# Eight experts on one core: three in plain fp32, woven between the five in split fp32

## The chip, the core and the metric

The kernel runs on one core of a Trainium2 chip, as one program. Its time is the device time of one execution in microseconds (us). Before the change it is 2560.36 us, the median of three runs (2557.41, 2560.36 and 2562.28).

Four engines matter here. TensorE (PE in the profile; its weight loads are PEld) multiplies out of SBUF into PSUM. VectorE (DVE) and ScalarE (ACT) do the elementwise work and bring PSUM back to SBUF. SyncE (SP) issues the DMAs that bring the weights from HBM, in the order of its queue.

## The reference

The model has two blocks of two layers each, on 256 tokens of width 1024. All but the last part is the same in both kernels and is not shown. The last part of the last layer is a mixture of eight experts, of which each token uses two:

```python
def moe_swiglu(h, router, w_gate, w_up, w_down):          # 8 experts, hidden width 3584
    t = h.reshape(-1, d)                                   # 256 tokens x 1024
    logits = (t @ router).astype(jnp.float32)
    top_v, top_i = lax.top_k(logits, TOP_K)                # TOP_K = 2
    top_w = jax.nn.softmax(top_v, axis=-1)
    gates = jnp.sum(jax.nn.one_hot(top_i, N_EXPERTS, dtype=jnp.float32) * top_w[..., None], axis=1)
    for e in range(N_EXPERTS):
        y_e = (jax.nn.silu(t @ w_gate[e]) * (t @ w_up[e])) @ w_down[e]
        out = out + gates[:, e:e + 1] * y_e
```

Each expert has three weight matrices of 1024 x 3584 fp32, 44 MB. All eight are read whole, 352 MB in all.

## The kernel before, in words

The kernel sorts the experts by the number of tokens that chose them. The first five places hold up to 128 tokens each, the last three up to 64 (`PLACES`); a branch at the end, which repeats the computation for tokens that didn't fit, is built into the program. `moe_gather` collects an expert's tokens with one-hot matmuls, `moe_places` transposes the one-hot matrix for the way back, and `combine` adds an expert's output to `acc`, scaled by the gate.

`moe_lane` is a generator. It walks through a list of experts, each in four steps over the hidden width (1024, 1024, 1024 and 512). A step takes its tokens through the gate matrix (`half(i, "gate")`), puts the SiLU into SBUF (`gate`), goes through the up matrix, multiplies (`inner`), transposes the product (`turn`) and takes it through the down matrix (`down`). The gate and up of step i + 1 stand ahead of the down of step i. It yields after each weight buffer. A weight buffer is 128 partitions x 2048 fp32, 1 MiB, and an expert has 42.

There are two kinds of experts:

- A wide one (places 0 to 4, 128 tokens) works in split fp32. `weights` (L211 to L229) loads a raw buffer, ScalarE casts it into a buffer wh (L227) and VectorE subtracts wh from raw into a buffer wl (L228). The raw buffer is then free. `mm3` makes three matmuls of each product (L242 to L244): twelve of 128x512 per weight buffer, each with 128 columns of the array.
- A tight one (places 5 to 7, 64 tokens) works in plain fp32. `whole_weights` (L231 to L237) loads a buffer, and TensorE reads it as it is, in four matmuls per weight buffer that use 64 columns each (L2307 for gate and up, L2364 for down). The profile counts each of these as two. The buffer is free when TensorE has read it.

The buffers of a kind form a ring: the code asks for them in turn, and the ring has five of raw and three each of wh and wl in this part of the kernel (`phase(2, 2, 48)`, `wider(raw=2, wh=1, wl=1)`, `wider(raw=1)`). A DMA can be issued when the buffer five turns earlier is free. The tight experts, which need no wh or wl, take the buffers of all three kinds in the order of `KINDS`, eleven in all.

PSUM has two pools of four banks, "a" and "b". Results of gate and up lie in "a", two banks for a wide expert and one for a tight one. Gathers, transposes, the results of down and the combines lie in "b".

`moe_pass` runs one lane over `TOGETHER`, the groups (0), (1, 2), (3, 4) and (5, 6, 7), so the five wide experts come first and the three tight ones last. A scheduler then sets the order of each engine's instructions by priority, near the order of the code.

Of the kernel before, what the change touches and what calls it, by code (L numbers as in the profile page):

```python
# [3 lines left out]

# [9 lines left out]
F32R = mybir.dt.float32r  # L14
# [8 lines left out]
D = 1024  # L23
# [5 lines left out]
def f(ap):  # L29
    return ap.bitcast(F32)  # L30
# [25 lines left out]
class Core:  # L56
# [171 lines left out]
                nc.vector.tensor_sub(L[:, c:e], raw[:, c:e], f(H[:, c:e]))  # L228
        return v(H), v(L)  # L229

    def whole_weights(s, src, k0, nk, c0, cn, rows="k p", kind="raw"):  # L231

        s.n += 1
        raw = s.buffer(kind)
        v = f(raw)[:, :nk * cn].rearrange("p (k c) -> p k c", k=nk)
        s.nc.sync.dma_start(v, src[k0:k0 + 128 * nk, c0:c0 + cn].rearrange(f"({rows}) c -> p k c", p=128))
        return v  # L237

# [1750 lines left out]
class MoE:  # L1989
# [192 lines left out]
                s.nc.sync.dma_start(s.out[t * 128:t * 128 + 128, c * 512:c * 512 + 512].rearrange(  # L2182
                    "p (d w) -> p d w", d=2), s.acc(t, c))

    def moe_gather(s, N, slot, js, places):


        nc = s.nc
        wide = places[js[0]] == 128
        n = len(js) * (2 if wide else 1)  # L2190
        j0, j1 = js[0], js[-1] + 1
        if wide:
            sl = s.small([128, 2, 4], "slotu")
            nc.vector.tensor_tensor(sl[:, :, :n].rearrange("p t (j u) -> p t j u", u=2),
                                    slot[:, :, j0:j1, None].to_broadcast([128, 2, j1 - j0, 2]),
                                    s.off[:, None, None, :].to_broadcast([128, 2, j1 - j0, 2]), op=OP.subtract)
            sl = sl[:, :, :n]
        else:
            sl = slot[:, :, j0:j1]
        P = s.t2([128, 2, 256], "onehot", F32R)  # L2200
        W = n * 64
        for t in range(2):
            nc.vector.tensor_tensor(P[:, t, :W].rearrange("p (u c) -> p u c", c=64), bc(s.slots[:, :64], n),
                                    sl[:, t, :, None].to_broadcast([128, n, 64]), op=OP.is_equal)
        X = []
        for d in range(0, ND, 2):
            p = s.psum("b")
            for m in range(2):
                for h, src in enumerate((N.H, N.L)):
                    for t in range(2):  # L2210
                        nc.tensor.matmul(p[:, m * W:m * W + W], src[d // 2][:, t, m * 128:m * 128 + 128], P[:, t, :W],
                                         start=(h == 0 and t == 0 and m == 0), stop=(h == 1 and t == 1),
                                         skip_group_check=True)
            if not wide:
                y = s.t2([128, 2, W], "xf")
            for m in range(2):
                v, g = p[:, m * W:m * W + W], s.col("ln_ffn_2", 8 + d + m)
                if wide:
                    x = s.t2([128, 512], "xe", F32R)[:, :2 * W].rearrange("p (a j c) -> p j a c", a=2, j=len(js))
                    v = v.rearrange("p (j c) -> p j c", j=len(js))  # L2220
                    nc.scalar.activation(x[:, :, 0], v, AF.Copy, scale=g)
                    nc.vector.scalar_tensor_tensor(x[:, :, 1], v, g, f(x[:, :, 0]), op0=OP.mult, op1=OP.subtract)
                    X.append(x)
                else:
                    nc.scalar.activation(y[:, m], v, AF.Copy, scale=g)
                    X.append(y[:, m].rearrange("p (j c) -> p j c", c=64))
        return {j: [X, i, places[j], P] for i, j in enumerate(js)}

    def moe_places(s, N, G):

        nc = s.nc
        rc = s.small([128, len(G)], "slotrc")
        p = s.psum("b")
        Y = []
        for X, i, n, P in G.values():
            y = P[:, :, i * n:i * n + n]
# [8 lines left out]
        nc.vector.tensor_copy(rc, p[:, :len(G)])  # L2245
        for g, y in zip(G.values(), Y):
            PT = s.t2([128, 2, 128], "onehotT", F32R)
            p = s.psum("b", dt=F32R)
            for t in range(2):
                nc.tensor.transpose(p[:, t * 128:t * 128 + 128], y[:, t], s.identR)  # L2250
            nc.scalar.copy(PT, p[:, :256].rearrange("p (t c) -> p t c", t=2))
# [1 line left out]

    AHEAD = 3
    WIDE = 1024
    KINDS = ("raw", "wh", "raw", "wl", "raw", "wh", "raw", "wl", "raw", "wh", "wl")

    def moe_weights(s, i):

# [1 line left out]

    def moe_pass(s, N, first, ahead):

        for _ in s.moe_lane(N, N.slot, s.PLACES, s.TOGETHER, first, ahead, True):
            pass

    def moe_lane(s, N, slot, places, together, G, ahead=(), most=False):


        nc = s.nc  # L2270
# [6 lines left out]
        py = {}  # L2277
        ahead = list(ahead)
        src = {nm: I[f"o_moe_w_{nm}_2"][0] for nm in ("gate", "up", "down")}
        kinds = itertools.cycle(s.KINDS)  # L2280

        def weights(nm, j, *a):
            e = N.expert[j]
            w = src[nm]
            w = w[e] if isinstance(e, int) else w[bass.ds(e, 1)].rearrange("o r c -> (o r) c")
            return s.weights(w, *a) if places[j] == 128 else s.whole_weights(w, *a, kind=next(kinds))

        def half(i, nm):

# [36 lines left out]
        def turn(i, h):  # L2326
# [2 lines left out]
            wide = G[steps[i][0]][2] == 128  # L2329
            out = []  # L2330
            for x in h:
                p = s.psum("b")
                n = x.shape[1] // 128
                for k in range(n):
                    nc.tensor.transpose(p[:, k * 128:k * 128 + 128], x[:, k // 2 * 256 + k % 2:k // 2 * 256 + 256:2],
# [32 lines left out]
        def combine(j):  # L2368
# [5 lines left out]
            for c in range(2):  # L2374
# [1 line left out]
                    yH, yL = s.t2([128, 512], "eyH", F32R), s.t2([128, 512], "eyL", F32R)  # L2376
                    s.split(py[j][c], yH, yL)
                for t in range(2):
                    p = s.psum("b")
                    if wide:  # L2380
                        mm(p, PT[:, t, :], yH, start=True, stop=False)
                        mm(p, PT[:, t, :], yL, start=False, stop=True)
# [6 lines left out]
        pg = yield from half(0, "gate")  # L2389
        if most:  # L2390
            s.moe_rms(N)
        s.moe_places(N, G)
        h = gate(0, pg)
        h = inner(0, h, (yield from half(0, "up")))
        for i in range(n):
            j, f0, fn = steps[i]
            if f0 == s.WIDE and i + per < n and steps[i + per][0] not in G:
                g = s.moe_gather(N, slot, next(x for x in together if steps[i + per][0] in x), places)
                s.moe_places(N, g)
                G |= g  # L2400
            pg = (yield from half(i + 1, "gate")) if i + 1 < n else None
            hs = turn(i, h)
# [62 lines left out]
```

## Time and profile before

The profile is of one execution; spans are from the first to the last instruction.

| | before |
|---|---|
| time of the profiled execution | 2560.47 us |
| its span | 2558.8 us |
| median of three runs | 2560.36 us |
| TensorE busy | 2382.6 us, 93% of the span |
| VectorE, ScalarE busy | 1679.8 us (66%), 1287.6 us (50%) |
| moved by DMA | 559.56 MB, 219 GB/s over the span |

In the profile's slices of 64 us each, TensorE stands at nine tenths or more nearly everywhere up to the last six slices, where it falls to seven or eight. The transfers rise from some 150 GB/s to about 350 GB/s at 1600 us, where the experts begin, and to about 410 GB/s in the last six slices. A share of busy time is an average; for what a stage is worth one reads which engine or transfer the others wait for in that stage. A matmul's busy time includes the time in which it passes through the array, which overlaps with the next one, so the distance of two starts says more than a duration. PEclk is the clock that TensorE was granted: 1.00 is 2.4 GHz.

### The profile page before, as it was taken

The page shows a single profiled execution, that of the slowest core. Times are in us where ns is not written, and L with a number is a line of the kernel's source. Part 1 is how long each engine was busy: PE and PEld are TensorE (multiplying, and loading weights), DVE is VectorE, ACT ScalarE, POOL GpSimd, SP SyncE. Part 2 cuts the span into 40 slices and gives each one's busy share as a digit, 9 for nine tenths or more (in the row PEclk, how much of TensorE's full clock was granted, in tenths as well). Part 3 has the DMA queues.
Part 4 walks back from the last instruction along what each step waited for, and adds up shares of the span by engine and source line. Part 5 has one row for each costly group of instructions (what it writes and reads, how often), then busy time and mean ns, then how long its engine had stood idle before and what let it go on. Part 6 is the DMA issues. An engine that isn't in the chain of part 4 may idle for free.

```text
span 2558.8 us, 39340 instructions
## 1 busy us (share of the span) xinstructions
PE 2382.6 (93%) x15516; PEld 2000.3 (78%) x15516; DVE 1679.8 (66%) x2974; ACT 1287.6 (50%) x2124; POOL 88.6 (3%) x180
## 2 busy tenths in 40 slices
PE   7988799999999999989999998999999999987786
PEld 6877689999888999879999898887888777632222
DVE  6876486658886765666657886888898988610000
ACT  4554265445555644664445553777777776510000
POOL 2011010000001000000000000000000000000000
PEclk9998699999999999989999998999999999999999
DMA  5310355555435455525554322899999998899998
GB/s 163 118 59 34 38 178 165 183 167 164 132 116 166 129 189 170 177 67 182 185 166 144 100 67 83 306 336 353 369 348 345 347 363 326 341 410 409 411 412 330
DMA packets 266191, 559.56 MB, mean 219 GB/s; under 512 B 12751, under 2 KB 172510, under 8 KB 251662
## 3 DMA queue, kind: packets, MB, share of 16 engines
q1 hardware_dynamic: 264544, 555.71, 61.3%
q0 software_dynamic: 1328, 1.22, 0.9%
q8 instruction: 124, 2.03, 0.3%
q14 instruction: 69, 0.57, 0.1%
q10 hardware_dynamic: 126, 0.03, 0.0%
HBM read 555.88 MB, written 1.05 MB: 218 GB/s over the span
## 4 chain that ended last, share of the span: by engine, by line
PE 71%; DMA 11%; DVE 8%; issue 4%; ACT 3%; POOL 2%; SPq 0%; ACTq 0%; POOLq 0%; DVEq 0%
PE pa L243 16%; PE pa L244 16%; PE pa L242 16%; DVE wl L228 3%; PE pb L243 3%; PE pb L244 2%; PE pb L242 2%; DMA raw<-in_o_moe_w_down_dram 2%; DMA wl<-in_o_moe_w_down_dram 2%; PE pb L1180 2%; PE pb L1805 2%; DMA wh<-in_o_moe_w_down_dram 2%; ACT wh L227 1%; PE pa L2307 1%; PE pb L1494 1%
## 5 line engine op out<-in xcount | busy, mean ns | idle before, releaser
L228 DVE TENSOR_TENSOR wl<-raw,wh 128x512 fp32r<-128x512 f32 (+1 forms) x982 | 974.4, 1021 | 204.3 <-ACT wh L227 199.9
L227 ACT CAST wh<-raw 128x512 fp32r<-128x512 f32 (+1 forms) x982 | 826.1, 888 | 549.7 <-issue 266.3
L242 PE MATMUL pa<-xH,wh 128*128 128x256 f32 (+1 forms) x1936 | 553.1, 286 | 16.0 <-ACT xH L326 8.1
L244 PE MATMUL pa<-xH,wl 128*128 128x256 f32 (+1 forms) x1936 | 552.9, 286 | 1.0 <-DVE wl L228 1.0
L243 PE MATMUL pa<-xL,wh 128*128 128x256 f32 (+1 forms) x1936 | 553.1, 286 | 0.6 <-DVE xL L327 0.5
L242 PEld LDWEIGHTS pa<-xH,wh 128*128 128x128 f32 (+1 forms) x1936 | 372.4, 193 | 18.2 <-ACT xH L326 8.8
L243 PEld LDWEIGHTS pa<-xL,wh 128*128 128x128 f32 (+1 forms) x1936 | 372.2, 192 | 3.5 <-DVE xL L327 2.0
L244 PEld LDWEIGHTS pa<-xH,wl 128*128 128x128 f32 (+1 forms) x1936 | 372.2, 192 | 2.9 <-DVE wl L228 1.9
L243 PE MATMUL pa<-wl,xe 128*128 128x512 f32 x560 | 220.9, 395 | 7.7 <-DVE wl L228 7.7
L244 PE MATMUL pa<-wh,xe 128*128 128x512 f32 x560 | 219.4, 392 | 0.0
L2323 DVE SCALAR_TENSOR_TENSOR eh<-pa,slotrc,eh 128x512 f32<-128x512 f32 (+1 forms) x47 | 33.4, 733 | 267.1 <-PE pa L2307 259.4
L242 PE MATMUL pa<-wh,xe 128*128 128x512 f32 x560 | 207.7, 393 | 0.0
L242 PE MATMUL pa<-hidH,wh 128*128 128x256 f32 x528 | 149.4, 283 | 0.0
L243 PE MATMUL pa<-hidL,wh 128*128 128x256 f32 x528 | 149.4, 283 | 0.0
L244 PE MATMUL pa<-hidH,wl 128*128 128x256 f32 x528 | 149.4, 283 | 0.0
L243 PEld LDWEIGHTS pa<-wl,xe 128*128 128x128 f32 x560 | 105.6, 189 | 33.9 <-DVE wl L228 12.8
L244 PEld LDWEIGHTS pa<-wh,xe 128*128 128x128 f32 x560 | 105.6, 189 | 21.1
L242 PEld LDWEIGHTS pa<-wh,xe 128*128 128x128 f32 x560 | 105.4, 189 | 21.2
L243 PE MATMUL pb<-wl,ehH 128*128 128x512 f32 x280 | 112.2, 401 | 1.5 <-DVE wl L228 1.5
L244 PE MATMUL pb<-wh,ehL 128*128 128x512 f32 x280 | 110.3, 394 | 0.0
L242 PE MATMUL pb<-wh,ehH 128*128 128x512 f32 x280 | 102.0, 393 | 2.5 <-ACT wh L227 2.5
L2317 ACT ACTIVATE eh<-pa,slotrc 128x512 f32<-128x512 f32 (+1 forms) x47 | 30.7, 674 | 145.3 <-PE pa L2307 125.8
(818 smaller groups left out, 3870.5 us busy)
## 6 DMA issues: line engine op xcount, KB each, us to landing
raw<-in_o_moe_w_down_dram SPq DMA_DIRECT2D x91, 1024.0 KB
raw<-in_o_moe_w_up_dram SPq DMA_DIRECT2D x89, 1024.0 KB
raw<-in_o_moe_w_gate_dram SPq DMA_DIRECT2D x88, 1024.0 KB
raw<-in_ffn_w_dram SPq DMA_DIRECT2D x60, 1024.0 KB
raw<-in_od_w_in_dram SPq DMA_DIRECT2D x20, 1024.0 KB
raw<-in_o_w_in_dram SPq DMA_DIRECT2D x16, 1024.0 KB
wl<-in_o_moe_w_gate_dram SPq DMA_DIRECT2D x13, 1024.0 KB
wh<-in_o_moe_w_up_dram SPq DMA_DIRECT2D x13, 1024.0 KB
```

The source lines that it names most:

```text
L227: nc.scalar.copy(H[:, c:e], raw[:, c:e])
L228: nc.vector.tensor_sub(L[:, c:e], raw[:, c:e], f(H[:, c:e]))
L242: mm(out, a[0], b[0], start=start, stop=False, skip_group_check=True)
L243: mm(out, a[0], b[1], start=False, stop=False, skip_group_check=True)
L244: mm(out, a[1], b[0], start=False, stop=stop, skip_group_check=True)
L1180: mm = lambda o, a, b, st=True, sp=True: nc.tensor.matmul(o, a, b, start=st, stop=sp, skip_group_check=True)
L1494: mm = lambda o, a, b, st, sp: nc.tensor.matmul(o, a, b, start=st, stop=sp, skip_group_check=True)
L1805: mm = lambda o, a, b, st=True, sp=True: nc.tensor.matmul(o, a, b, start=st, stop=sp, skip_group_check=True)
L2307: mm(p[0][64 * c:64 * c + 64, :hw], X[k0 + k][:, u], w[:, k, c * hw:c * hw + hw], start=start, stop=stop, skip_group_check=True)
L2317: nc.scalar.activation(out[-1], p, AF.Silu, scale=rc)
L2323: nc.vector.scalar_tensor_tensor(x, p, rc, x, op0=OP.mult, op1=OP.mult)
```

## The change

`moe_pass` makes two lanes of the one. Lane a walks through the five wide experts, lane b through the three tight ones. After `LEAD` = 8 weight buffers of lane a, the tight experts' tokens are gathered; from then on, whenever the count is due, lane b takes `BURST` = 4 weight buffers in one go. With 202 wide buffers left and 126 tight ones this is a burst after every six or seven wide buffers.

The tight lane's transposes, gathers and combines take their PSUM banks from pool "a" (`side="a"`); its down results stay in "b". `whole_weights` takes raw buffers alone, so `KINDS` is gone: both lanes now share the five raw buffers. Lines from L229 on shift (the cast is L226 and the subtraction L227 after the change, the tight matmuls L2323 and L2380).

```diff
-    def whole_weights(s, src, k0, nk, c0, cn, rows="k p", kind="raw"):
+    def whole_weights(s, src, k0, nk, c0, cn, rows="k p"):
...
-        raw = s.buffer(kind)
-        v = f(raw)[:, :nk * cn].rearrange("p (k c) -> p k c", k=nk)
+        v = s.buffer("raw")[:, :nk * cn].rearrange("p (k c) -> p k c", k=nk)
...
-    KINDS = ("raw", "wh", "raw", "wl", "raw", "wh", "raw", "wl", "raw", "wh", "wl")
+    LEAD = 8
+    BURST = 4
...
     def moe_pass(s, N, first, ahead):
 
-        for _ in s.moe_lane(N, N.slot, s.PLACES, s.TOGETHER, first, ahead, True):
-            pass
+        wide = [x for x in s.TOGETHER if s.PLACES[x[0]] == 128]
+        tight = [x for x in s.TOGETHER if s.PLACES[x[0]] == 64]
+        a = s.moe_lane(N, N.slot, s.PLACES, wide, first, ahead, True)
+        per = 3 * D * s.FE // (128 * 2048)
+        na, nb = per * sum(map(len, wide)), per * sum(map(len, tight))
+        for _ in range(s.LEAD):
+            next(a)
+        na -= s.LEAD
+        b = s.moe_lane(N, N.slot, s.PLACES, tight, s.moe_gather(N, N.slot, tight[0], s.PLACES, "a"), side="a")
+        due = 0
+        for _ in range(na):
+            next(a, None)
+            due += nb
+            if due >= s.BURST * na:
+                due -= s.BURST * na
+                for _ in range(s.BURST):
+                    next(b, None)
+        for x in (a, b):
+            for _ in x:
+                pass
...
-    def moe_lane(s, N, slot, places, together, G, ahead=(), most=False):
+    def moe_lane(s, N, slot, places, together, G, ahead=(), most=False, side="b"):
...
-            return s.weights(w, *a) if places[j] == 128 else s.whole_weights(w, *a, kind=next(kinds))
+            return s.weights(w, *a) if places[j] == 128 else s.whole_weights(w, *a)
...
-                p = s.psum("b")
+                p = s.psum(side)
```

On TensorE, before the change, the first tight matmuls follow the last but one buffer pair of the wide experts. Here xf are the tight experts' tokens; raw_22583, wh_22589 and so on are weight buffers that TensorE reads as they are (numbers count allocations):

```order
L243 MATMUL pb_22014<-wl_22566,ehH_22466 128x512
L244 MATMUL pb_22014<-wh_22565,ehL_22467 128x512
L2307 MATMUL pa_22582<-raw_22583,xf_22099 64x512 x4
L2307 MATMUL pa_22582<-wh_22589,xf_22111 64x512 x4
L2307 MATMUL pa_22582<-raw_22595,xf_22123 64x512 x4
L2335 MATMUL pb_22607<-ident,eh_22470 128x128 x4
L2307 MATMUL pa_22582<-wl_22601,xf_22135 64x512 x4
L2307 MATMUL pa_22618<-raw_22619,xf_22099 64x512 x4
```

From there on the tight buffers follow each other to the end. After the change, an early burst on TensorE, between a wide expert's up (xe its tokens) and its down (ehH its hidden values), reads:

```order
L242 MATMUL pa_18708<-wh_18764,xe_17894 128x512
L2323 MATMUL pa_18782<-raw_18783,xf_18157 64x512 x3
L2323 MATMUL pa_18782<-raw_18789,xf_18169 64x512 x4
L2323 MATMUL pa_18782<-raw_18795,xf_18181 64x512 x4
L2351 MATMUL pb_18952<-ident,eh_18703 128x128 x4
L2351 MATMUL pb_18961<-ident,eh_18705 128x128 x4
L2323 MATMUL pa_18782<-raw_18801,xf_18193 64x512 x4
L240 MATMUL pb_18395<-wh_18810,ehH_18690 128x512
```

Four tight buffers stand between two wide ones, one of their matmuls a little ahead within the wide buffer before, and the wide expert's own transposes (L2351) fall between them.

In the DMA queue on SP, before the change, the tight buffers' DMAs cycle through three kinds of buffers. In brackets stands whose semaphores the DMA waits for (DMAHW are earlier DMAs):

```order
L236 DMA raw_22583<-in_o_moe_w_gate_dram 128x2x1024 [waits DMAHW1_49,DVE_49]
...
L236 DMA wh_22589<-in_o_moe_w_gate_dram 128x2x1024 [waits DVE_49,PE_49]
...
L236 DMA raw_22595<-in_o_moe_w_gate_dram 128x2x1024 [waits DMAHW2_49]
...
L236 DMA wl_22601<-in_o_moe_w_gate_dram 128x2x1024
...
L236 DMA raw_22619<-in_o_moe_w_up_dram 128x2x1024 [waits DMAHW3_49]
```

After the change the queue at the first burst is this; L221 are wide buffers, L234 tight ones:

```order
L221 DMA raw_18332<-in_o_moe_w_up_dram 128x2x1024 [waits DMAHW7_49,DVE_49]
L234 ISA
L234 DMA raw_18351<-in_o_moe_w_gate_dram 128x2x1024 [waits DMAHW0_49,DVE_49]
...
L234 DMA raw_18369<-in_o_moe_w_gate_dram 128x2x1024 [waits DMAHW3_49,DVE_49]
L221 DMA raw_18375<-in_o_moe_w_up_dram 128x2x1024 [waits DMAHW4_49,DVE_49]
L221 DMA raw_18397<-in_o_moe_w_down_dram 128x2048 [waits DMAHW5_49,PE_49]
L221 DMA raw_18415<-in_o_moe_w_down_dram 128x2048 [waits DMAHW6_49,PE_49]
L221 DMA raw_18433<-in_o_moe_w_down_dram 128x2048 [waits DMAHW7_49,PE_49]
L221 DMA raw_18451<-in_o_moe_w_down_dram 128x2048 [waits DMAHW0_49,PE_49]
L221 DMA raw_18553<-in_o_moe_w_gate_dram 128x2x1024 [waits DMAHW1_49,DVE_49]
```

The burst's own DMAs and the first wide one behind it wait for VectorE; the four wide DMAs after that wait for TensorE to have read the four tight buffers. This pattern repeats 31 times, and two tight buffers are left for the end.

## Rows read from the trace of the kernel before

**Rows 1.** Windows: length, busy us (instructions) of PE, PEld, DVE, ACT, POOL, PEclk, DMA share, GB/s.

```profile
1598.40:2222.00 623.60, 614.44 (x2810) 506.34 (x2809) 537.26 (x357) 445.52 (x326) 0.70 (x1) 1.00 0.92 341
2222.00:2548.00 326.00, 264.43 (x1199) 87.36 (x1198) 23.23 (x29) 20.77 (x32) 0.00 (x0) 0.99 1.01 405
2250.00:2500.00 250.00, 206.38 (x933) 66.36 (x933) 15.97 (x23) 13.44 (x23) 0.00 (x0) 1.00 1.02 410
2240.00:2250.00 10.00, 5.99 (x16) 3.77 (x13) 5.34 (x3) 3.80 (x2) 0.00 (x0) 0.69 1.02 410
```

**Rows 2.** Waits of SP's DMA queue, 1600 to 2222: total us, times, longest.

```profile
SPq L222 <- DVE wl L228: 466.1, 193, 8.3
```

**Rows 3.** ScalarE's time line: start, duration, instruction, [idle before <- releaser].

```profile
1860.08 1.92 ACT L227 CAST wh<-raw 128x2048 fp32r<-128x2048 f32 x1 [0.82 <-PE pa L244]
1862.80 1.92 ACT L227 CAST wh<-raw 128x2048 fp32r<-128x2048 f32 x1 [0.81 <-PE pa L244]
```

**Rows 4.** Groups of instructions, 1650 to 2200: count | busy us, mean ns | idle before.

```profile
L228 DVE TENSOR_TENSOR wl<-raw,wh 128x2048 fp32r<-128x2048 f32 x184 | 416.8, 2288 | 57.4 <-ACT wh L227 56.3
L227 ACT CAST wh<-raw 128x2048 fp32r<-128x2048 f32 x184 | 350.6, 1913 | 92.2 <-PE pa L244 51.2 <-PE pb L244 31.7 <-DVE eyL L304 5.9
```

**Rows 5.** TensorE's time line where the stages meet, 2222 to 2229.

```profile
2221.72 0.39 PE L244 MATMUL pb<-wh,ehL 128*128 128x512 f32 x1
2222.04 1.94 PE L2307 MATMUL pa<-raw,xf 128*64 128x512 f32 x8
2223.81 1.89 PE L2307 MATMUL pa<-wh,xf 128*64 128x512 f32 x8
2225.52 1.89 PE L2307 MATMUL pa<-raw,xf 128*64 128x512 f32 x8
2227.34 0.74 PE L2335 MATMUL pb<-ident,eh 128*128 128x128 f32 x4
2228.01 1.51 PE L2307 MATMUL pa<-wl,xf 128*64 128x512 f32 x6
```

**Rows 6.** Groups on TensorE, 2222 to 2559: transposes and combines.

```profile
L2335 PE MATMUL pb<-ident,eh 128*128 128x128 f32 x46 | 9.5, 316 | 4.7 <-DVE eh L2323 4.7
L2384 PE MATMUL pb<-ey,onehotT 64*128 64x512 f32 x24 | 6.0, 615 | 2.1 <-ACT ey L2373 2.1
```

**Rows 7.** Short windows around an empty stretch of the transfers.

```profile
1852.40:1856.40 4.00, 4.00 (x18) 3.00 (x16) 1.29 (x1) 3.80 (x4) 0.00 (x0) 1.00 1.02 423
1857.60:1858.40 0.80, 0.80 (x4) 0.67 (x5) 0.80 (x1) 0.80 (x1) 0.00 (x0) 1.00 0.18 72
1859.60:1863.60 4.00, 4.00 (x19) 3.29 (x19) 3.96 (x3) 2.72 (x2) 0.00 (x0) 1.00 1.03 398
```

**Rows 8.** SP's time line there: DMA issues (merged, xcount).

```profile
1849.38 3.07 SPq L222 DMA_DIRECT2D raw<-in_o_moe_w_down_dram  x2
1857.43 7.28 SPq L222 DMA_DIRECT2D raw<-in_o_moe_w_gate_dram  x4
```

**Rows 9.** TensorE's time line at the last wide pair, inside the tight stage.

```profile
2243.29 0.85 PE L242 MATMUL pb<-wh,ehH 128*128 128x512 f32 x2 [2.53 <-ACT wh L227]
2245.61 0.79 PE L243 MATMUL pb<-wl,ehH 128*128 128x512 f32 x1 [1.48 <-DVE wl L228]
2246.20 0.63 PE L244 MATMUL pb<-wh,ehL 128*128 128x512 f32 x1
2246.63 0.63 PE L243 MATMUL pb<-wl,ehH 128*128 128x512 f32 x1
```

**Rows 10.** TensorE's time line at the first wide matmul.

```profile
1598.48 0.77 PE L242 MATMUL pa<-wh,xe 128*128 128x512 f32 x1
```

**Rows 11.** Time line of the end: last down matmul, last combine, stores.

```profile
2545.88 1.94 PE L2364 MATMUL pb<-raw,ehT 128*64 128x512 f32 x8 [0.44 <-DMA raw<-in_o_moe_w_down_dram]
2548.50 1.99 PE L2384 MATMUL pb<-ey,onehotT 64*128 64x512 f32 x8 [0.69 <-ACT ey L2373]
2550.44 2.96 SPq L2182 DMA_DIRECT2D out_dram<-hT  x4
```

More of the change, by code (lines that the diff above doesn't have):

```diff
@@ L1 @@
-import itertools
 import math
@@ L2183, in moe_store, with moe_gather @@
                     "p (d w) -> p d w", d=2), s.acc(t, c))
-    def moe_gather(s, N, slot, js, places):
+    def moe_gather(s, N, slot, js, places, side="b"):
         nc = s.nc
@@ L2227, in moe_gather, with moe_places @@
         return {j: [X, i, places[j], P] for i, j in enumerate(js)}
-    def moe_places(s, N, G):
+    def moe_places(s, N, G, side="b"):
         nc = s.nc
         rc = s.small([128, len(G)], "slotrc")
-        p = s.psum("b")
+        p = s.psum(side)
         Y = []
@@ L2247, in moe_places @@
             PT = s.t2([128, 2, 128], "onehotT", F32R)
-            p = s.psum("b", dt=F32R)
+            p = s.psum(side, dt=F32R)
             for t in range(2):
@@ L2279, in moe_lane @@
         src = {nm: I[f"o_moe_w_{nm}_2"][0] for nm in ("gate", "up", "down")}
-        kinds = itertools.cycle(s.KINDS)
         def weights(nm, j, *a):
@@ L2331, in turn @@
             for x in h:
-                p = s.psum("b")
+                p = s.psum(side)
                 n = x.shape[1] // 128
@@ L2378, in combine @@
                 for t in range(2):
-                    p = s.psum("b")
+                    p = s.psum(side)
                     if wide:
@@ L2391, in moe_lane @@
             s.moe_rms(N)
-        s.moe_places(N, G)
+        s.moe_places(N, G, side)
         h = gate(0, pg)
@@ L2397, in moe_lane @@
             if f0 == s.WIDE and i + per < n and steps[i + per][0] not in G:
-                g = s.moe_gather(N, slot, next(x for x in together if steps[i + per][0] in x), places)
-                s.moe_places(N, g)
+                g = s.moe_gather(N, slot, next(x for x in together if steps[i + per][0] in x), places, side)
+                s.moe_places(N, g, side)
                 G |= g
```

## The prediction

> **What bounds the kernel now.** I read the table of windows by stage first, then the waits of the DMA queue, then the time line of single engines at the two places where the stages meet. The experts are the last 960 us of the span and fall into two stages with opposite limits [rows 1]. In the first, 1598.4 to 2222.0, the five wide experts run: TensorE is busy for 614 of 623.6 us at a granted clock of 1.00, while the transfers move 341 GB/s. In the second, 2222 to 2548, the three tight experts run: the transfers stand at a share of 1.01 and 405 GB/s (410 in its undisturbed middle), and TensorE's busy share falls to 264 of 326 us. In the first stage the DMA queue waits 466.1 us, in 193 waits, for a raw buffer that VectorE's subtraction gives back [rows 2]: transfers wait for buffers there, and buffers for TensorE. I call a wide weight buffer W and a tight one T; each is 1 MiB. By the code there are 42 per expert, so 210 W and 126 T.
>
> A steady W costs TensorE 2.72 us: successive casts start at 1860.08 and 1862.80, each released by TensorE [rows 3]. With everything that belongs to it (transposes, gathers, combining, the slow start) it is 623.6 us / 208 = 3.00 us, since two of the 210 come later. In front of it lie a cast of 1.91 and a subtraction of 2.29 us [rows 4]. A T looks like 1.94 us, but the starts of three that stand back to back, 2222.04, 2223.81 and 2225.52, are 1.71 to 1.77 us apart [rows 5]; I take 1.72. A T therefore leaves TensorE about a third of its transfer's 2.56 us (1.0486 MB at 410 GB/s), and a W asks for more than its transfer gives. That is the room the change works in.
>
> **The change part by part.** Within the two stages 0.341 x 623.6 + 0.405 x 326.0 = 344.7 MB are moved [rows 1]. At 410 GB/s that is 841 us: the floor by transfers. The floor by TensorE is a sum of four terms.
> - 210 W: 623.6 us as measured, and two more at 2.72: 629 us.
> - 126 T at 1.72: 217 us.
> - What the tight lane does beside them: 42 of the 46 transposes (the other four are of a wide expert) at 0.67 per four, from 2227.34 to 2228.01 [rows 5], 7 us; and three combines of 2.0 us [rows 6, 11]: 6 us. Together 13 us.
> - Changes between 128 and 64 columns. In the program order TensorE changes its tile shape 146 times from the first tight matmul on, before 44 times. Two changes can be priced: the W at 2221.72 is followed by a T after 0.32 instead of the 0.227 of a twelfth of 2.72, and the third T, which ends its four steps of 0.43 at 2227.24, by a transpose at 2227.34 [rows 5]. Both cost 0.1 us; 102 more changes make 10 us.
>
> Sum: 869 us, against 949 us from the first W at 1598.48 to the end of the last T at 2547.8 [rows 10, 11]. TensorE, not the transfers, will set the pace, by 3%.
>
> The Trainium skill, page TensorEngine Tiling (Array Packing), section Tiling Modes, speaks against the interleaving: a change of the tiling mode, as opposed to the tile, drains TensorE. The trace agrees that there is a cost, 0.1 us at the two places [rows 5]. If each drain cost a whole W matmul of 0.39 us instead [rows 5], 102 changes would make 40 us and the sum 899.
>
> The waits come on top. The tight lane loses six buffers: before, a T could lie in five raw, three wh or three wl buffers, now in the five raw alone, which it shares with W. A raw buffer under a T comes free only when TensorE has read it, and the queue, which is in order, then holds back all that follows. So I follow one burst with the ring full, time 0 at the first T: T2 to T4 and W1 lie in the other four buffers. T1 is read at 1.8. From a restart at 1857.43 after an empty stretch [rows 8] the rate is 72 GB/s a little later and 398 from 1859.6 [rows 7]: 2.0 us from issue to flow. So W2 lands at 1.8 + 2.0 + 2.6 = 6.4, is cast by 8.3 and subtracted by 10.6. TensorE has finished the four T at 7.0 and W1 at 9.8; it can start W2 on the cast half (two matmuls, 0.45 us) and waits 0.3. W3 needs the buffer of T2 (3.5), lands at 9.0, is subtracted by 13.2, and TensorE arrives at 13.0. So a burst costs 0.3 us if the ring is full when it starts. If it is not, and TensorE takes every W as soon as it is split, W1 comes 12.8 us of transfers after the W before the burst, is ready at 9.8 by the same clock, and the wait is 2.8; but then transfers run without a pause and the 841 us hold. From the other side a burst may also gain a little, since its 7 us let ScalarE and VectorE, which are full for 446 and 537 of 624 us [rows 1], catch up. Bounds per burst: -0.3 to 2.8; I take 0.5, near the full ring, and for 31 bursts 15 us. (SiLU and PSUM copies of the tight lane, 0.6 to 0.7 us on ScalarE, now stand between casts; they are in the 0.5.)
>
> The gathering of the three tight experts moves from the wide stage's end to its start and takes the four banks of the other PSUM pool; nothing is saved or added. The end, from the last T to the end of the span, stays 11.0 us [rows 11]: the last thing issued is still a tight expert's combine and the stores.
>
> So: 1598.5 + 869 + 15 + 11 = 2493.5 us of span. The profiled execution took 2560.47 with a span of 2558.8, 1.7 more, and the median before is 2560.36, the same. Forecast: 2495 us, 65 us or 2.6% less.
>
> **The rivals.**
> 1. *Transfers set the end.* If waits vanish and T, W and changes cost less than I think, 841 us of transfers remain: 1598.5 + 841 + 11 + 1.7 = 2452, and with some 15 us of lost starts 2467. For it: slices at 423 and 398 GB/s while casts and subtractions run [rows 7]. Against it: 869 is a sum of measured paces.
> 2. *Every burst ends as the W pair inside the tight stage does now.* There TensorE waits 2.53 for the cast and 1.48 for the subtraction, and then runs at 1.2 GHz (clock 0.69 in these 10 us, matmuls 0.43 instead of 0.227 apart) [rows 1, 9]. Price: 4.0 us, and 12 x 0.2 = 2.4 for one W at the slow clock. Place: the first W that has to be loaded after a burst. 31 x 6.4 = 198 us, a time near 2680. It decides from (949 - 869) / 31 = 2.6 us per burst on: above that the kernel is slower. For it: the ring is smaller than the eleven buffers, and my margins at W2 and W3 are a few tenths. Against it: that pair lay behind seven T with nothing split ahead, whereas here up to three W are. A half of it, 2 us a burst, gives 2540.
> 3. *The wide stage's rate is a ceiling, not a lack of buffers.* If transfers cannot pass 341 GB/s beside casts and subtractions, 344.7 MB take 1011 us and the end is at 2622; it decides below 344.7 / 949 = 363 GB/s. Against it: the slices of 398 and 423 GB/s at full clock and with splits running [rows 7].
> 4. *The engines' order stays as it was.* Excluded: the DMA queue's order shows six or seven W, then four T, 31 times, and TensorE's the same.
>
> The Trainium skill's page DMA: Bandwidth & Descriptors, section Specifications, gives a limit of about 358 GB/s of HBM per core, by which the transfers would take 344.7 / 0.358 = 963 us and the time would be 2574, slower. The 410 GB/s held for 250 us [rows 1] contradict it, for this core.
>
> **How the numbers follow.** Forecast with its range of waits 0.75; rival 1 0.10; the half of rival 2 0.05; rival 2 past its deciding point 0.05; rival 3 0.03; within 0.2%, which is about what measurements of this kernel can tell from no change (5 us), 0.02. So faster 0.90, same 0.02, slower 0.08. The forecast's own ends: without waits and changes 859 us, 2470; with 1.5 us a burst and 0.39 a change 945 us, 2556 if both come together, 2535 with one of them and half the other. The range for 8 in 10 is 2462 to 2540.
>
> **What would show it.** Right: one stage from 1600 on, with TensorE busy nearly throughout and transfers near 390 GB/s; TensorE's waits a few tenths of a us at the second and third W of a burst; clock 1.00. Wrong: clock below 0.95 in stretches of that stage (rival 2); a DMA share of 1.0 at under 365 GB/s (rival 3); or waits of TensorE for DMA in the T themselves, which would mean that the ring of five is too short for four T and not for the W behind them.

## The result: slower by 1.8%

The changed kernel takes 2604.94 us (median of four runs, 2599.63 to 2609.19) against 2560.36: a ratio of 1.0177, 95% interval 1.0155 to 1.0199. The forecast was 2495 us, with a chance of 0.08 for slower. The profiled execution took 2601.64 us.

| | after |
|---|---|
| span | 2599.8 us |
| TensorE busy | 2422.1 us, 93% |
| VectorE, ScalarE busy | 1683.3 us (65%), 1285.8 us (49%) |
| moved by DMA | 559.56 MB, 215 GB/s |
| expert stage, first wide matmul to last matmul | 999.1 us (1592.47 to 2591.59), before 952.0 (1598.48 to 2550.49) |

The first wide matmul comes 6 us earlier, although the change doesn't touch the part before it; in this execution that part ran at 1.2 GHz for 109 instead of 130 us. So I compare the lengths of the stage.

The change does what it says: one stage instead of two. Windows of after (columns as in [rows 1]):

```profile
1592.47:2591.59 999.12, 928.05 (x4015) 608.87 (x4015) 564.81 (x387) 465.77 (x358) 0.70 (x1) 0.97 0.91 345
1700.00:2500.00 800.00, 743.09 (x3167) 480.82 (x3168) 448.74 (x277) 365.06 (x263) 0.00 (x0) 0.98 0.94 359
2323.10:2329.90 6.80, 6.04 (x14) 4.78 (x15) 5.11 (x3) 3.35 (x3) 0.00 (x0) 0.50 1.02 372
```

The transfers move 359 GB/s, not 390; TensorE is busy 93% of the time, not nearly throughout; and the clock falls to 1.2 GHz in ten short stretches (the third row is one); with the tail of an earlier one at the stage's start that is 51 us, before 10. TensorE's waits in the stage, and those of the DMA queue (who waits for whom: total us, times, longest):

```profile
PE pa L241 <- DVE wl L227: 37.0, 28, 2.6
PE pa L240 <- ACT wh L226: 13.4, 8, 3.6
PE pb L241 <- DVE wl L227: 11.2, 15, 1.6
PE pb L240 <- ACT wh L226: 3.1, 2, 2.5
```

```profile
SPq L234 <- DVE wl L227: 294.8, 122, 5.0
SPq L221 <- PE pa L2323: 222.4, 84, 14.6
SPq L221 <- DVE wl L227: 157.8, 62, 6.0
SPq L221 <- PE pb L2380: 86.6, 38, 6.4
```

64.7 us of TensorE's waits, the four lines together, are for casts and subtractions, which I call the splits: 2.1 us a burst. None of note is for a transfer in the tight matmuls. In the queue, where [rows 2] had one line, the wide DMAs (L221) now wait 309 us (222.4 + 86.6) for TensorE to read tight buffers.

To see where 47 us went I sorted the distances between the starts of successive matmuls of the stage, in this and in every later run: steady distances (0.227 for wide, 0.43 for a pair of tight halves, 0.12 for a transpose), what comes on top at half clock, within eight matmuls of a change of shape, and in gaps over 0.3 us (waits). "Halves alone" is what tight halves cost that don't start side by side with their partner. The time is the median of a kernel's runs; the stage and all right of it are of its one profiled execution, in us.

| run | time | ratio (95%) | stage | halves alone | changes: number, us | half clock | waits |
|---|---|---|---|---|---|---|---|
| before | 2560.4 | | 952.0 | 1.7 | 44, 10 | 4 | 89 |
| after | 2604.9 | 1.016-1.020 | 999.1 | 19.6 | 142, 28 | 21 | 82 |
| e1 bursts of 2 | 2640.8 | 1.029-1.036 | 1026.8 | 41.3 | 232, 47 | 17 | 72 |
| e2 bursts of 1 | 2694.8 | 1.050-1.056 | 1084.0 | 90.3 | 480, 89 | 8 | 49 |
| e3 bursts of 8 | 2596.0 | 1.010-1.017 | 990.1 | 13.5 | 104, 19 | 30 | 84 |
| e4 before, ring of 5 | 2565.7 | 1.000-1.003 | 955.9 | 1.7 | 44, 10 | 4 | 93 |
| e5 order kept | 2596.0 | 1.011-1.016 | 984.7 | 1.7 | 92, 17 | 22 | 92 |
| e6 pieces 1024 | 2560.1 | 0.998-1.001 | 950.6 | 5.7 | 120, 23 | 5 | 63 |
| e7 ring of 4 | 2688.1 | 1.047-1.052 | 1081.1 | 19.6 | 142, 28 | 59 | 127 |
| e8 e5 + e6 | 2568.8 | 1.002-1.005 | 956.1 | 1.7 | 108, 19 | 10 | 71 |
| e9 e1 + e5 | 2596.7 | 1.013-1.018 | 988.2 | 0.9 | 130, 25 | 20 | 89 |
| e10 pieces 512 | 2538.3 | 0.991-0.995 | 928.8 | 2.6 | 102, 22 | 4 | 45 |
| e11 e3 + e6 | 2558.0 | 0.997-1.001 | 947.5 | 3.7 | 82, 16 | 14 | 64 |
| e12 e9 + e6 | 2601.9 | 1.016-1.020 | 987.8 | 0.9 | 130, 25 | 19 | 88 |
| e13 copies behind | 2617.6 | 1.022-1.027 | 1012.2 | 15.3 | 130, 26 | 23 | 94 |
| e14 e10 + e13 | 2594.8 | 1.012-1.017 | 986.2 | 6.0 | 110, 21 | 22 | 86 |
| e15 e10, copies placed apart | 2547.7 | 0.992-0.997 | 939.0 | 4.7 | 108, 22 | 4 | 49 |
| e16 before, pieces 512 | 2578.7 | 1.006-1.009 | 969.4 | 0.9 | 40, 10 | 3 | 102 |
| e17 e10, ring of 7 | 2533.0 | 0.986-0.991 | 922.5 | 3.4 | 102, 21 | 5 | 40 |
| e18 e17, bursts of 8 | 2516.4 | 0.980-0.985 | 906.5 | 1.7 | 78, 14 | 4 | 34 |

The 89 us of before are mostly waits for transfers in its tight stage (51 us in nine lines; the longest two are below), which the weaving did take away.

```profile
PE pa L2307 <- DMA raw<-in_o_moe_w_up_dram: 10.6, 15, 1.2
PE pa L2307 <- DMA wh<-in_o_moe_w_up_dram: 7.8, 12, 0.9
```

But others took their place. The first full burst of after (the DMA queue, ScalarE, VectorE, TensorE; columns as in [rows 3]):

```profile
1642.32 5.48 SPq L221 DMA_DIRECT2D raw<-in_o_moe_w_down_dram  x4
...
1647.58 1.91 ACT L226 CAST wh<-raw 128x2048 fp32r<-128x2048 f32 x1 [3.72 <-DMA raw<-in_o_moe_w_down_dram]
1651.00 1.91 ACT L226 CAST wh<-raw 128x2048 fp32r<-128x2048 f32 x1 [1.51 <-DMA raw<-in_o_moe_w_down_dram]
1653.48 1.91 ACT L226 CAST wh<-raw 128x2048 fp32r<-128x2048 f32 x1 [0.57 <-DMA raw<-in_o_moe_w_down_dram]
...
1649.52 2.29 DVE L227 TENSOR_TENSOR wl<-raw,wh 128x2048 fp32r<-128x2048 f32 x1 [3.34 <-ACT wh L226]
...
1640.35 7.09 PE L2323 MATMUL pa<-raw,xf 128*64 128x512 f32 x32
...
1650.21 0.62 PE L240 MATMUL pb<-wh,ehH 128*128 128x512 f32 x2
...
1651.87 0.50 PE L241 MATMUL pb<-wl,ehH 128*128 128x512 f32 x1 [0.33 <-DVE wl L227]
```

Counted from the burst's start, the wide DMA that waits for the first tight read is issued at 1.97 (predicted 1.8). Its cast starts as it lands, at 7.23 (6.4), the subtraction ends at 11.46 (10.6), and the next wide weight is there not 2.6 but 3.4 us later. TensorE reaches the cast half at 9.86 (9.8) and would wait 1.2 us; here it fills most of that with six gather matmuls. From the DMA's issue to the finished split it is 9.5 us, and the work that TensorE has for that time, three tight buffers and one wide, covers 7.9.

### The profile page after: what moved, and what is told of

It is laid out like the page before. It is cut to its first block, busy times and chain, and to the rows that moved or that the text cites. A ratio compares the mean times of both kernels' runs of the same rounds, so it can differ in the third digit from the quotient of the medians.

```text
span 2599.8 us, 39321 instructions
## 1 busy us (share of the span) xinstructions
PE 2422.1 (93%) x15516; PEld 2007.7 (77%) x15516; DVE 1683.3 (65%) x2974; ACT 1285.8 (49%) x2124; POOL 88.0 (3%) x180
## 2 busy tenths in 40 slices
DMA packets 266191, 559.56 MB, mean 215 GB/s; under 512 B 12751, under 2 KB 172510, under 8 KB 251662
## 4 chain that ended last, share of the span: by engine, by line
PE 71%; DVE 11%; ACT 5%; DMA 4%; issue 4%; POOL 2%; ACTq 0%; POOLq 0%; DVEq 0%; SPq 0%
PE pa L241 16%; PE pa L242 15%; PE pa L240 15%; DVE wl L227 5%; PE pa L2323 4%; ACT wh L226 3%; PE pb L241 2%; DMA raw<-in_o_moe_w_down_dram 2%; PE pb L2380 2%; PE pb L242 2%; PE pb L1178 2%; PE pb L240 2%; PE pb L1803 1%; PE pb L1492 1%; PE pb L1144 1%
## 5 line engine op out<-in xcount | busy, mean ns | idle before, releaser
L227 DVE TENSOR_TENSOR wl<-raw,wh 128x512 fp32r<-128x512 f32 (+1 forms) x982 | 975.9, 1021 | 366.0 <-ACT wh L226 361.6
L226 ACT CAST wh<-raw 128x512 fp32r<-128x512 f32 (+1 forms) x982 | 824.6, 887 | 724.0 <-issue 266.8
L241 PE MATMUL pa<-wl,xe 128*128 128x512 f32 x560 | 230.7, 412 | 37.1 <-DVE wl L227 37.0
L242 PE MATMUL pa<-wh,xe 128*128 128x512 f32 x560 | 224.8, 401 | 0.0
L240 PE MATMUL pa<-wh,xe 128*128 128x512 f32 x560 | 212.1, 406 | 13.4 <-ACT wh L226 13.4
L2323 PE MATMUL pa<-raw,xf 128*64 128x512 f32 (+1 forms) x768 | 169.3, 548 | 1.8 <-ACT ehT L2360 1.4
L240 PEld LDWEIGHTS pa<-wh,xe 128*128 128x128 f32 x560 | 107.5, 195 | 48.2 <-ACT wh L226 18.9
L242 PEld LDWEIGHTS pa<-wh,xe 128*128 128x128 f32 x560 | 108.9, 194 | 21.5
L2323 PEld LDWEIGHTS pa<-raw,xf 128*64 128x64 f32 x768 | 56.0, 137 | 90.0 <-issue 78.2
```

The costliest lines, as they stand in the source:

```text
L226: nc.scalar.copy(H[:, c:e], raw[:, c:e])
L240: mm(out, a[0], b[0], start=start, stop=False, skip_group_check=True)
L241: mm(out, a[0], b[1], start=False, stop=False, skip_group_check=True)
L242: mm(out, a[1], b[0], start=False, stop=stop, skip_group_check=True)
L2323: mm(p[0][64 * c:64 * c + 64, :hw], X[k0 + k][:, u], w[:, k, c * hw:c * hw + hw], start=start, stop=stop, skip_group_check=True)
```

## Experiments

**e1, e2, e3: other bursts.** `BURST = 2`, `1` and `8` instead of 4.

> BURST = 2: 63 bursts of two tight buffers instead of 31 of four. A (ring of five): the wide buffer whose DMA waits for the first tight read is now the fourth behind a burst, not the second; the cover is 1.7 + 3 x 2.7 = 9.9 us against some 9.3 from issue to subtracted (5.1 landing + 1.9 + 2.3), where four left 1.7 x 3 + 2.7 = 7.9. So the 65 us of TensorE's waits on the wide splits and the 20 us lost at 1.2 GHz go, 63 more pairs of shape changes cost 6: 2605 - 85 + 6 = 2526 us. B (casts held up on ScalarE behind the lanes' PSUM copies): as many copies as before, 2605 within 10. C (transfers can't pass 365 GB/s beside casts): 344.7 MB / 0.365 = 944 us, no end before 1592 + 944 + 13 = 2549. D (a shape change costs 1.0 us, not 0.1): 63 more pairs, well above 2605, near 2670.

> BURST = 1: 126 single tight buffers. A: cover 4 x 2.7 = 10.9 us, no lack; 190 more shape changes than with four at 0.1 = 19 us: 2605 - 85 + 19 = 2539 us. B: 2605 within 10, plus 19 for changes. C: not before 2549. D (1.0 us a change): 2790.

> BURST = 8: 16 bursts of eight, longer than the ring. A: the first wide DMA behind a burst waits for the fourth tight read; cover 4 x 1.7 = 6.9 us against 9.3, lack 2.4 us, more than the 1.4 of four, but half as often: about 16 x 3.5 with the slow clock behind it = 55 instead of 85, and half the changes: 2605 - 30 - 3 = 2572 us, slower than bursts of two, faster than of four. B: 2605 within 10. C: between 2549 and 2605. D (1.0 us a change): 2605 - 31 = 2574, the same as A, which the runs with 1 and 2 tell apart.

Measured 2640.8, 2694.8 and 2596.0: the ring theory (A) has the wrong sign for small bursts. Only D, a price of 1.0 us a change, had the sign, and it was too high (2670 and 2790). What rises there is in the table: halves alone and changes. e3 missed A's 2572 and D's 2574 and lies within 10 us of B's 2605. But in e3 most waits on splits begin, followed back, at a late landing, 58 of 75 us (in after 16 of 72; these sums go by distances between starts, so they are a little above the 64.7), as the ring theory says of bursts longer than the ring. TensorE's time line of e2 shows the halves:

```profile
2115.97 0.62 PE L240 MATMUL pb<-wh,ehH 128*128 128x512 f32 x2
2116.53 1.07 PE L2380 MATMUL pb<-raw,ehT 128*64 128x512 f32 x2
2117.53 0.50 PE L241 MATMUL pb<-wl,ehH 128*128 128x512 f32 x1
2117.87 0.39 PE L242 MATMUL pb<-wh,ehL 128*128 128x512 f32 x1
...
2119.70 0.39 PE L242 MATMUL pb<-wh,ehL 128*128 128x512 f32 x1
2120.02 1.93 PE L2380 MATMUL pb<-raw,ehT 128*64 128x512 f32 x6
```

A tight product has two halves of 64 columns, which start together and share 0.43 us. The scheduler put two halves between a wide buffer's matmuls on wh and those on wl, and their partners ten wide matmuls later: 1.0 us up to the next wide matmul for work worth 0.43, and the tight buffer stays occupied 2.5 us longer. Behind a change the second wide matmul follows after 0.34 instead of 0.227: the price of a change isn't all in its first distance. Over the stage of after it is 28 / 142 = 0.2 us, in e1 (47 / 232) and e2 (89 / 480) about the same.

**e4: the loss of six buffers alone.** `KINDS = ("raw",)` in the kernel before.

> The kernel before with its tight experts in the five raw buffers alone (KINDS = raw), not woven: the loss of six buffers by itself. A: the five buffers matter only where a burst has to hide a wide load, cast and subtraction; a tight buffer's landing of 5.1 us is covered by five of 2.56, so the tight stage stays at 405 GB/s and the time at 2560 within 5 us. Rival (the tight experts need the eleven buffers to keep the transfers full): the tight stage longer, by 10 to 30 us.

2565.7, an interval of 1.000 to 1.003: at the edge of the first theory's 5 us, and short of the rival's 10 to 30.

**e5, e6, e8: order and pieces.** e5 keeps the wide and tight matmuls in the order of the code:

```diff
+    def inline(s, i):
+        if s.token:
+            s.tc.stamp_issue_order_token(i.ins, s.token)
...
+            s.inline(mm(out, x, y, start=st, stop=sp, skip_group_check=True))
...
+                            s.inline(mm(p[0][64 * c:64 * c + 64, :hw], X[k0 + k][:, u], w[:, k, c * hw:c * hw + hw],
...
```

e6 splits in two pieces, and e8 does both:

```diff
-        s.piece = 2048
+        s.piece = 1024
         first = s.moe_gather(N, s.byexp[:, 0:2], (0,), s.PLACES)
```

> Bursts of four; the wide and the tight matmuls of TensorE keep the order of the code (the scheduler may only move the others between them). P (parted pairs and changes): the scheduler has put wide matmuls between the two 64-column halves of a tight product, which in the stage before run side by side in 0.43 us; each parted half costs 0.43 by itself. In the traces 96 halves stand alone after the change, 200 with bursts of two, 432 with one, 66 with eight: 20, 41, 90 and 13.5 us more than in pairs; and a change of shape and back costs 0.4 us, with 71, 116, 240 and 52 of them. Kept in order, nearly all pairs and some 40 changes come back: 2605 - 20 - 16 = 2569 us. A and B (waits alone): the waits of 65 us stay, 2605 within 8.

> The wide weights are cast and subtracted in two pieces of 1024 columns instead of one of 2048 in the expert stage, else as after. L (latency from landing to the first wl matmul): it falls from 1.9 + 2.3 = 4.2 us to about 2.1, and from issue of the DMA from 9.3 to 7.2, below the cover of 7.9 us that three tight buffers and one wide give: most of the 65 us of waits on the splits goes and with it the stretches at 1.2 GHz: about 2605 - 50 - 12 = 2543 us. B (casts stand behind the lanes' PSUM copies in ScalarE's queue, which wait for TensorE): only the subtraction's half is saved, about 1 us in 31 bursts, 2575. C (transfers stay at 365 GB/s): not below 2590, since the transfers, not the splits, set the pace.

> Both the kept order and the pieces of 1024. If P and L add up: 2605 - 36 - 62 = 2507 us, faster than before. If only P holds: 2569; if the transfers are the limit (C): not below 2560.

e5: the halves came together and the changes fell, 29 us, but a third came back as waits; the stage is 14 us shorter, the time 9. That is neither P's 2569 nor the 2605 within 8 of waits alone. e6: 2560.1, near the middle between theory L's 2543 and B's 2575; the waits fell by 19 us, the loss at half clock by 16, and the halves by 14, in the order that the scheduler now chose. So not all of e6's gain is shorter latency. e8: 2568.8. That is the number of "only P", by luck, since P alone had given 2596.0 in e5; the two don't add up, and with pieces the kept order loses 9 us against e6 (waits 71 instead of 63).

**e7: a ring of four.** Without `with s.wider(raw=1)`.

> Four raw buffers instead of five, else as after: a burst then fills the whole ring, and the first wide DMA behind it waits for the first tight read. A (ring): the cover shrinks by one wide buffer, 2.7 us, in each of 31 bursts: 2605 + 84 = 2690 us. B, P (ScalarE's queue, parted pairs): 2605 within 15. C (rate of the transfers): 2605 within 10.

2688.1, the ring theory's 2690. The sum is another than the theory's, which had all 84 us as waits: in the table the waits rise by 45 us and the loss at half clock by 38. TensorE's waits on the splits rise from 64.7 to 105.7 us and 1.2 GHz holds for 150 us instead of 51:

```profile
PE pa L240 <- ACT wh L226: 41.1, 21, 3.6
PE pa L241 <- DVE wl L227: 38.2, 27, 1.8
PE pb L241 <- DVE wl L227: 14.3, 10, 1.6
PE pb L240 <- ACT wh L226: 12.1, 9, 2.5
```

**e9 to e12.** e9 is e1 with e5's order; e10 has pieces of 512, e11 e6 with bursts of eight, e12 e9 with pieces of 1024.

> Bursts of two (2640.8 us as the scheduler orders them) with the matmuls of TensorE kept in the order of the code. P (parted halves and changes): the 200 halves that stand alone there, 41 us, come together, and of 232 changes some 100 go, 20 us: 2580 us. A (ring) on top: once the order is kept, the cover of 9.9 us behind a burst of two shows, and most of the 72 us of waits and 17 us at the slow clock go as well: 2520. A alone, without P: 2640. T (transfers and TensorE are both nearly full, and what one gains the other takes): 2570 to 2600.

> Bursts of four, casts and subtractions in four pieces of 512 columns (two pieces of 1024 gave 2560.1 us). L (latency from landing to the first wl matmul): 2.1 us becomes about 1.1, so TensorE's remaining 31 us of waits on wl and 13 on wh halve: 2540 us. T (transfers are the limit now: their share is 0.97 to 1.01 in most windows of the run with two pieces): 2560 within 6.

> Bursts of eight with pieces of 1024. A with L: the first wide DMA behind a burst waits for the fourth tight read, cover 4 x 1.72 = 6.9 us against 7.2 from issue to the first wl: lack 0.3 us in 16 bursts, and some 40 changes fewer at 0.2: 2560 - 8 - 5 = 2547. T: transfers stand at the limit only while the ring turns, and eight reads in a row give it less to do: 2560 to 2575. Without a part of the ring in it (P alone): 2552.

> Bursts of two, order kept, pieces of 1024: all three together. A, P and L added: cover 9.9 us against 7.2, no parted halves, some 130 changes at 0.2 = 26 us, so little is left but the floors: about 2515 us, faster than both. T (transfers at 380 to 400 GB/s beside casts, 344.7 MB in 862 to 907 us, and what is lost where the two take turns): 2545 to 2565.

e10 gives 2538.3, what L said, and is the first to beat before. Its splits (count | busy, mean ns):

```profile
L227 DVE TENSOR_TENSOR wl<-raw,wh 128x512 fp32r<-128x512 f32 x766 | 473.8, 688 | 139.0 <-ACT wh L226 137.1
L226 ACT CAST wh<-raw 128x512 fp32r<-128x512 f32 x764 | 414.1, 620 | 225.7 <-DMA raw<-in_o_moe_w_down_dram 90.0 <-DMA raw<-in_o_moe_w_gate_dram 70.4 <-DMA raw<-in_o_moe_w_up_dram 50.5
```

The first piece is ready 1.3 us after the landing (0.62 + 0.69) instead of 4.2, and the raw buffer is free after about 3.4 (0.62 + 4 x 0.69). The Trainium skill says it in Perfetto Trace Analysis, section Optimizing Scalar/DVE Operations: where these engines aren't full but cause bubbles on others, breaking up instructions may let work be done sooner. The trace agrees, and e16 below shows the condition in it. e11 (2558.0) is nearest to T's 2560: what bursts of eight save against e6 in changes and halves, 9 us, they lose again at half clock, 9 us (of their waits on splits 37 of 51 us begin at landings). e9 and e12 failed for bursts of two: with the order kept the halves are gone, but 89 and 88 us of waits stay, where the ring theory had them go. e9's 2596.7 lies in T's range, e12's 2601.9 in none. In their queue the tight DMAs wait for tight reads, which those of after hardly do (e9):

```profile
SPq L221 <- DVE wl L227: 366.1, 158, 6.5
SPq L234 <- PE pa L2331: 198.2, 75, 7.3
SPq L234 <- PE pb L2388: 113.0, 37, 7.4
```

With three or four wide buffers between two bursts, five turns back from a tight buffer lies mostly another tight one; the queue is in order, so the wide DMAs behind stand too. That fits, but was not tested by itself.

**e13 to e16.** Followed back from each wait on a split, 54 of 72 us in after begin at a PSUM copy or product of a lane that stands before the casts and waits for TensorE. e13 lets the next cast or subtraction pass the tight lane's SiLU, product and copy, and the next two pass the wide lane's ehH and ehL:

```diff
+                s.tc.add_manual_dep(x[0].ins, ab[x[1]].ins.name, mybir.DependencyInfo(
+                    mybir.DependencyClass.NoSync, mybir.DependencyReason.DATA))
...
-                nc.scalar.activation(out[-1], p, AF.Silu, scale=rc)
+                i = nc.scalar.activation(out[-1], p, AF.Silu, scale=rc)
+                if side == "a":
+                    s.late(i, 0)
```

e14 has it with pieces of 512. e15 instead puts off the tight lane's products, transposes and combines by four wide buffers and a burst by one where a wide half has just ended (`if due >= s.BURST * na and not last:`). e16 is before with pieces of 512.

> As after (bursts of four, whole casts), but in the queues of ScalarE and VectorE the tight lane's SiLU, product and copy stand one wide cast (or subtraction) later, and the wide lane's ehH and ehL two later. B (the heads of these queues wait for TensorE while landed weights lie behind them: 54 of 72 us of waits): with one or two splits let through first, half of these 54 us and half of the 21 us at the slow clock go: 2605 - 27 - 10 = 2568 us, and waits that begin at ehH fall from 31 to under 12 us. A (late landings alone): 2605 within 8, since a cast can't be earlier than its landing; or slower, if the transposes' banks come free later.

> The same with pieces of 512 (2538.3 us without it). B: of the 30 us of split waits left there 22 begin at such copies; half of them go: 2538 - 11 = 2527 us. T (transfers at 385 to 411 GB/s with a share of 1.0 are the limit by now): 2538 within 5.

> Pieces of 512; the tight lane's products, transposes and combines are put into the program four wide buffers behind a burst instead of at its edges, and no burst directly follows the end of a wide half (so the wide lane's own PSUM work comes before it). Another way to the same end as e14. B: 2538 - 11 to 15 = 2525 us. T: 2538 within 5. If PSUM banks held longer by the tight lane matter: above 2545.

> The kernel before, not woven, with pieces of 512 in its expert stage. There TensorE is busy for 614 of 624 us of the wide stage and the transfers bound the tight one, so shorter splits have little to give: 2560 - 5 = 2555 at best (the 10 us around the wide pair in the tight stage). Then some 17 of the 22 us by which e10 beats before belong to the weaving. Rival: the pieces alone give it, 2540.

The theory fell: 2617.6, 2594.8 and 2547.7, none faster than without. (e15's 2547.7 is past the 2545 that its third expectation names for PSUM banks; its runs spread from 2538 to 2554, and the banks were not tested.) ScalarE's waits, first in after, then in e13:

```profile
ACT wh L226 <- DMA raw<-in_o_moe_w_down_dram: 106.2, 37, 11.9
ACT ehH L299 <- PE pb L2351: 85.5, 19, 13.5
ACT wh L226 <- DMA raw<-in_o_moe_w_gate_dram: 64.6, 38, 10.0
ACT ehT L2360 <- PE pa L2351: 62.7, 11, 13.0
ACT wh L226 <- DMA raw<-in_o_moe_w_up_dram: 56.3, 16, 10.1
```

```profile
ACT wh L226 <- DMA raw<-in_o_moe_w_up_dram: 155.4, 47, 12.9
ACT wh L226 <- DMA raw<-in_o_moe_w_down_dram: 130.2, 52, 11.4
ACT wh L226 <- DMA raw<-in_o_moe_w_gate_dram: 123.7, 49, 11.9
...
ACT ehH L2378 <- PE pb L2373: 16.0, 8, 3.5
```

The copies hardly wait now, but the casts wait for landings, 409 instead of 227 us, and TensorE's waits on splits stay at 64 us; followed back in the same way, 62 of these begin at a landing. The chain back had led to the last waiter, not to the cause. e14 loses more against its base (56 us against e10, where e13 loses 13 against after): a copy behind a cast waits for that cast's landing, and TensorE for the copy (19 us for ehT).

e16 (2578.7) missed both its expectations, 19 us slower than before. Its subtractions:

```profile
L228 DVE TENSOR_TENSOR wl<-raw,wh 128x512 fp32r<-128x512 f32 x711 | 435.8, 682 | 32.3 <-ACT wh L227 31.8
```

Four times 0.682 are 2.73 us a wide buffer, as long as TensorE's 2.72. The loss lies in the wide stage (641 instead of 624 us), where VectorE is busy for 494 of the 550 us from 1650 to 2200, in before for 476. So VectorE seems to become a second bound there, and woven it would have the bursts to catch up; no run tests that by itself. What is measured is that pieces alone lose 19 us, weaving alone 45, and that at equal pieces the weaving gains 40 (2578.7 to 2538.3).

**e17, e18: seven raw buffers.** The split rings shrink to two each in this stage, in the same space; e18 has bursts of eight.

```diff
-    AHEAD = 3
+    AHEAD = 2
...
-                    with s.wider(raw=1):
-                        s.moe(N)
+                s.ring = {nm: r[:2] for nm, r in s.ring.items()}
...
+                with s.wider(raw=5):
+                    s.moe(N)
```

> As e10 (2538.3 us: bursts of four, pieces of 512), with seven raw buffers and two each of wh and wl instead of five and three each, in the same space (two of the first splits are made ahead instead of three). A (the ring): of the 45 us of waits there 31 are on the splits; two more buffers cover them by 5 us a burst, so most go: 2538 - 20 = 2518 us. T (the transfers' rate, 385 to 411 GB/s with a share of 1.0): 2538 within 5. If two split buffers are too few, TensorE waits for a split at every wide buffer: above 2560.

> The same with bursts of eight. A: the first wide DMA behind a burst waits for the second tight read, cover 6 x 1.72 = 10.3 us against about 6.2 from issue to the first split piece: no lack, and some 40 changes of shape at 0.2 us less: e17 - 8 us, about 2510. T: the same as e17 within 5. If the ring is still too short for eight: e17 + 10.

e17: 2533.0, at the edge of T's 2538 within 5; A's 2518 failed, and the intervals of e10 and e17 overlap. e18: 2516.4, the fastest here, 1.8% below before (0.980 to 0.985) and 17 us below e17, where A had 8. Its window, and its waits on splits:

```profile
1700.00:2500.00 800.00, 779.34 (x3523) 523.04 (x3523) 534.80 (x869) 460.01 (x852) 0.00 (x0) 1.00 1.00 396
```

```profile
PE pb L241 <- DVE wl L227: 6.7, 10, 1.2
PE pa L240 <- ACT wh L226: 6.1, 9, 0.7
PE pa L241 <- DVE wl L227: 4.9, 11, 1.0
```

Transfers at 396 GB/s, TensorE busy 97%, clock 1.00: what the prediction had said of the first version.

## Why the prediction was wrong

The stage was to last 869 + 15 + 3 = 887 us and lasted 999. Point by point:

- *Wide buffers, tight pairs, transposes and gathers*: foreseen 642 + 217, measured 216.5 for the tight pairs and 632 for the rest (what the 999 us leave when these and the table's four columns are taken off). Right. So was the disappearance of the waits for transfers in the tight work. The sum has the last combine twice, in the 13 us of the tight lane and in the 11 us of the end, which is 2 us too much.
- *Changes of shape, 10 us for 102 more*: the number is right (142 in the trace, 146 in the order), the price was read from the first distance behind a change alone [rows 5]; it is 0.2 each, and all 142 make 28 us, 18 more than the 10.
- *Halves alone*: a term that was missing, 20 us. The order had shown single tight matmuls ahead of their burst; I counted them as changes and did not ask what a half costs without its partner.
- *Waits, 0.5 us a burst*: this is the step that failed. They are 2.1 (64.7 us in 31 bursts), inside my bounds of -0.3 to 2.8, but I took a value near the wrong end. The margin of 0.3 us hung on 4.6 us from issue to landing, taken from when a window's rate had recovered [rows 7, 8], and on one landing every 2.6 us at once. The first burst has 5.3 and then 3.4; in the twelve places of after where a wide DMA is issued over 5 us behind the one before and its cast waits for it, 4.8 to 6.8 us pass up to the cast. So the wide weights behind a burst come later than TensorE. e7 supports the mechanism (83 us for one buffer less), e6 and e10 support it from the side of the latency, e4 shows that it is the mixture, not the smaller ring as such; against it stand e1, e9 and e12, where bursts of two keep their waits. By the gaps, waits are 67 us more than foreseen, gathers and others included.
- *Slow clock*: I had put it into rival 2 alone. In [rows 1, 9] TensorE ran at 1.2 GHz behind two waits of 2.53 and 1.48 us. In after the granted clock fell to that level ten times, nine of them in or right behind one or two waits of 1.6 to 3.6 us, once behind waits of 0.5 alone, and behind two waits of over 2 us (2.15 and 2.38) it did not. With the tail at the stage's start that lost 21 us. Waits and clock together are (64.7 + 20.7) / 31 = 2.75 us a burst, just past the 2.6 from which that rival decides. Its 0.05 was far too little for a case whose margins were, as I wrote, a few tenths.

These come to 18 + 20 + 67 + 21 - 13 = 113 us, against 112 that were missing (the 13 are 642 + 217 and the 3 us of the end, less 632 + 216.5). Rival 1 did not occur. Rival 3 is refuted by e18, which moves 396 GB/s over 800 us beside all casts and subtractions: so the 359 of after were no ceiling. Rival 4 was excluded rightly. Nor does the limit of about 358 GB/s of the Trainium skill's page DMA: Bandwidth & Descriptors, section Specifications, hold for this core: e18's 396 GB/s lie above it.

Open: what holds bursts of two at 2597 to 2602 us with the order kept (the ring theory is not the whole account of the waits); how much of after's 65 us comes from tight buffers held longer by parted halves (e5 undid the parting, and the waits rose); and what e18's last 34 us of waits are.

## What to carry to other kernels

When two streams share one ring, follow a buffer from its release over issue, landing and conversion to its first use, with times from a lone transfer and not from a full pipe, and compare that with the work that covers it; where margins are tenths, give the failing side real weight. A long wait at the end of a chain of queues need not be its cause: take it away and see whether the next one takes its place. Pieces shorten such a chain, if the converting engine has room for their overhead. With pieces, seven raw buffers at the cost of one converted buffer of each kind gave 5 us at bursts of four, hardly clear of the noise, and together with bursts of eight 22.

## What the runs showed of the hardware

- Two 64-column matmuls side by side take 0.43 us for both (before); one by itself takes as long (e2).
- The price of a change between 128- and 64-column matmuls is spread over the next ones, some 0.2 us in sum, in 142 changes (after, 28 us) as in 480 (e2, 89 us).
- In the first burst of after a 1 MiB transfer issued into an empty queue lands 5.3 us later, the next one 3.4 after it, and the third 2.5 after that.
- Cutting 128x2048 into 128x512 makes VectorE's subtraction 2.73 (e16, 4 x 0.682) instead of 2.29 us in sum, ScalarE's cast 2.48 (e10, 4 x 0.620) instead of 1.91.
